# First norm with squares and splits on VectorE alone, in the text's order, and the first two mixer strips part by part together

## The chip, the cores and the metric

The kernel runs on one core of one Trainium2 chip. A core has TensorE (PE, matrix products; PEld loads its weights), VectorE (DVE), ScalarE (ACT), GpSimd (POOL) and SyncE (SP, which here only issues transfers), and 16 DMA engines. The metric is the device time of one execution in microseconds; lower is better. The profile is of one execution taken by the hardware profiler, in us from its first instruction.

## The reference, cut to what matters

One step of a one-layer hybrid decoder for 1024 prompt tokens and 8 × 4 sample tokens with the same weights. The first stages are what the change touches: keys and values of a memory of 256 tokens, the first norm, and the projection of the normed tokens.

```
def rmsnorm(x, g):
    var = jnp.mean(xf * xf, axis=-1, keepdims=True)
    return xf * lax.rsqrt(var + EPS) * g

p_mem_k = jnp.einsum('bmd,lde->lbme', mem_prompt, w_mem_k)
p_mem_v = jnp.einsum('bmd,lde->lbme', mem_prompt, w_mem_v)
...
u = rmsnorm(h, W['norm_mix'][l])
proj = jnp.einsum('bld,de->ble', u, W['w_in'][l])     # columns: pool | z | x,B,C | dt | gate | lru
xbc, new_conv = causal_dwconv(xbc, conv_buf, conv_w, conv_b)   # width 4, then SiLU
...
```

Behind it come three mixers (pooling, a state-space scan, a recurrent block), the output projection, attention to the memory and a SwiGLU layer; the change leaves them as they are.

## The kernel before, in words

**Layout and products.** The 1056 tokens (1024 prompt, 32 sample) lie along the free axis; the 1024 features are 8 tiles of 128 partitions, `xs[0]` to `xs[7]`. The columns are worked in three **parts** `c` of 352. An fp32 operand is split in two fp32r numbers, a high half (a copy on ScalarE) and a low half (the value less the high half, a subtraction elsewhere), and each product becomes three: high·high, high·low, low·high. A **unit** (L146 to L158) is the 8 × 3 products of one strip of 128 output features with one part (or with the memory); it calls `tick()` at its half and at its end, which counts time for work started with `spawn` (generators that go on after so many ticks).

**Memory keys and values.** `w_kv` has 16 weight tiles of 128x1024. `issue` loads one into one of six buffers, `split` makes its halves. Eight key units (the loop over `m`, bank `pk`, then a copy `kt` on ScalarE) use tiles 0 to 7; then eight **value groups** (the loop over `k`, 12 products of 128x512 each) sum into four banks `pvv` with tiles 8 to 15. Ahead of each unit or group `beside(i)` runs: it loads token tile `i − 1`, issues weight tile `i + 5`, splits tile `i + 1`, and squares a token tile: ScalarE makes the square, VectorE or GpSimd adds it to `acc`. After the last square `rstd_all` is spawned: sums of `acc` over the features on TensorE (`pv`, L251), the reciprocal root on VectorE, and transposes (`pb`, L322) that ScalarE copies to `rbc`, the norm factor of each token.

**Norm and splits.** `norm_x(c)` makes for each feature tile of part `c` the normed value in place (L330, VectorE), its high half `uh` (L331, ScalarE) and its low half `ul` (L332; VectorE for even tiles, GpSimd for odd ones). Between part 0 and the others the four banks of values are copied out (`vn`, L388 on ScalarE and L390 on VectorE) and stored (L391, issued by ScalarE).

**Projection.** `xbc_proj` takes the strips of x, B and C in the order 8, 10, 0, 1, 2, 3. For each strip and part there is one unit (bank `mm`, three buffers) and then `conv_unit`: a copy `raw` and a scaled copy `cy` on ScalarE, three steps on VectorE (L503), the tanh on ScalarE. Ahead of strip 8's three units stands `dt_unit`, the time steps: 16 products with `dpad`, L427. Weights of the strips come one ahead (`one_ahead`), with two buffers for the halves and three for what is loaded.

**What sets the order.** TensorE and SyncE run in the order of the program's text all through. VectorE and ScalarE do so up to L382, in the block `kv_order`; elsewhere, and on GpSimd all through, a scheduler orders what is ready in its model.

Of the kernel before, what the change touches and what calls it, by code (L numbers as in the profile page):

```python
# [9 lines left out]
F32 = mybir.dt.float32  # L10
F32R = mybir.dt.float32r
AF = mybir.ActivationFunctionType
OP = mybir.AluOpType
PSUM = bass.MemoryType.PSUM

P = 128
# [3 lines left out]
CW = 352  # L20
NCH = 3
LASTP = SEQ - 2 * CW
DM = 1024
KD = DM // P
# [35 lines left out]
def hybrid_step(ctx, tc, xT, memT, consts_d, masks_d, wbd_d, poolw_d, spool_d, w_kv, w_xbc, w_dt, w_lg, w_pool, w_z, h0_d,  # L60
                w_out1, w_out2, w_q, kc_d, vc_d, w_o, w_gu, w_down,
                yT, ktT, vN, smallo, pssd, sssd):
    nc = tc.nc
# [11 lines left out]
    def nm(s):  # L75
        cnt[0] += 1
        return f"{s}{cnt[0]}"

    def slot(dt=F32, name="s"):
        return sl.tile([P, T], dt, tag="slot", name=nm(name))  # L80
# [5 lines left out]
    def spawn(gen):  # L86
        step(gen)
# [38 lines left out]
    def strips():  # L126

        lists = [(w_xbc[m], DM) for m in (8, 10, 0, 1, 2, 3, 9, 11, 4, 5, 6, 7)]
        lists += [(w_pool[g], DM) for g in range(4)]
        lists += [(w_lg[4 * j + t], DM) for t in range(4) for j in range(2)]  # L130
        lists += [(w_z[m], DM) for m in range(8)]
        lists += [(w_out2[m], DM) for m in range(8)] + [(w_out1[m], DM) for m in range(8)]
        lists += [(w_q[m], DM) for m in range(8)]
        lists += [(w_o[0, m], 512) for m in range(8)]
        yield from one_ahead(lists)
# [9 lines left out]
    weights = strips()  # L145

    def unit(out, w, xs, cols, kk):
        whi, wlo = w
        for k in range(kk):
            a, b = k * P, k * P + P  # L150
            xh, xl = xs[k]
            nc.tensor.matmul(out, whi[:, a:b], xh[:, cols], start=k == 0, stop=False)  # L152
            nc.tensor.matmul(out, whi[:, a:b], xl[:, cols], start=False, stop=False)  # L153
            nc.tensor.matmul(out, wlo[:, a:b], xh[:, cols], start=False, stop=k == kk - 1)  # L154
            if k == kk // 2 - 1:
                tick()
        tick()

    def ch(c):
        return slice(c * CW, (c + 1) * CW)  # L160
# [7 lines left out]
    def cc(name, i=None, n=1):  # L168
        a, b = COFF[name]
        return cst[:, a:b] if i is None else cst[:, a + i:a + i + n]  # L170
# [49 lines left out]
    def square_into(acc, src, first, tmp, eng=nc.gpsimd):  # L220
        if first:
            nc.scalar.activation(acc, src, AF.Square)
        else:
            nc.scalar.activation(tmp, src, AF.Square)
            eng.tensor_tensor(acc, acc, tmp, op=OP.add)
# [11 lines left out]
    tp = mx_.enter_context(tc.tile_pool(name="tp", bufs=2))  # L237
# [3 lines left out]
    def so(name):  # L241
        a, b = SOFF[name]
        return outs[:, a:b]
# [14 lines left out]
    kv_order = ExitStack()  # L258
# [4 lines left out]
    raws = [slot(name="kvw")[:, :DM] for _ in range(6)]  # L263
# [42 lines left out]
    u = []  # L306
    rb0 = slot(name="rbc")
    acc = slot(name="acc")
    xs = []
# [15 lines left out]
    def norm_x(c):  # L325
        if c == 0:
            u.extend((slot(F32R, "uh"), slot(F32R, "ul")) for _ in range(KD))
        for k in range(KD):
            x, (hi, lo) = xs[k][:, ch(c)], u[k]
            nc.vector.scalar_tensor_tensor(x, x, cc("gmix", k), rb0[:, ch(c)], op0=OP.mult, op1=OP.mult)  # L330
            nc.scalar.activation(hi[:, ch(c)], x, AF.Copy)  # L331
            (nc.gpsimd if k % 2 else nc.vector).tensor_tensor(lo[:, ch(c)], x, hi[:, ch(c)].bitcast(F32), op=OP.subtract)  # L332

    def beside(i):

        if 0 <= i - 1 < KD:
            x = slot(name="x")
            nc.sync.dma_start(x, xT[(i - 1) * P:(i - 1 + 1) * P, :])
            xs.append(x)
        if i + 5 < 16:  # L340
            issue(i + 5)
        if i + 1 < 16:
            split(i + 1)
        k = i - 1 - 2
        if 0 <= k < KD:
            square_into(acc, xs[k], k == 0, slot(name="sq") if k else None, nc.vector if k > 4 else nc.gpsimd)
        if k == KD - 1 + 2:
            spawn(rstd_all())

    for m in range(8):  # L350
# [12 lines left out]
    pv = [ps.tile([P, 512], F32, tag="mm", name=nm("pvv"), bufs=3) for _ in range(3)] + [smps(name="pvv")]  # L363
    for k in range(KD):
        beside(8 + k)
        if k == 3:
            nc.sync.dma_start(cst, consts_d)
            nc.sync.dma_start(msk, masks_d)
            nc.sync.dma_start(wdt, w_dt)
        whi, wlo = kvw[8 + k]  # L370
        for i in range(2):
            for j in range(2):
                a, e = slice(i * P, (i + 1) * P), slice(j * 512, (j + 1) * 512)
                hi, lo = mpairs[k]
                nc.tensor.matmul(pv[2 * i + j], hi[:, a], whi[:, e], start=k == 0, stop=False)
                nc.tensor.matmul(pv[2 * i + j], lo[:, a], whi[:, e], start=False, stop=False)
                nc.tensor.matmul(pv[2 * i + j], hi[:, a], wlo[:, e], start=False, stop=k == KD - 1)
        tick()
    nc.scalar.activation(dpad3[:, :, :16], wdt3, AF.Copy)
    nc.vector.tensor_tensor(dpad3[:, :, 32:48], wdt3, dpad3[:, :, :16].bitcast(F32), op=OP.subtract)  # L380
    drain()
    kv_order.close()  # L382
    norm_x(0)
    for i in range(2):
        for j in range(2):
            vn = sd.tile([P, 512], F32, tag="seg", name=nm("vn"), bufs=4)
            if j:
                nc.scalar.activation(vn, pv[2 * i + j], AF.Copy)  # L388
            else:
                nc.vector.tensor_copy(vn, pv[2 * i + j])  # L390
            nc.scalar.dma_start(vN[i * P:(i + 1) * P, j * 512:j * 512 + 512], vn)  # L391
    for c in range(1, NCH):
        norm_x(c)

    def softplus(p, x, n):

# [93 lines left out]

    def conv_unit(c, psum, conv_i, sstate, pout, sout, prev, y):

        raw = tp.tile([P, 3 + CW], F32, tag="raw", name=nm("raw"), bufs=3)
        if c == 0:
            nc.gpsimd.memset(raw[:, :3], 0.0)
        else:
            nc.gpsimd.tensor_copy(raw[:, :3], prev[:, CW:CW + 3])
        w = [cc("conv", conv_i * 5 + j) for j in range(5)]
        n = CW if c < 2 else LASTP
        nc.scalar.activation(raw[:, 3:], psum, AF.Copy)  # L500
        nc.scalar.activation(y, psum, AF.Identity, scale=w[3], bias=w[4])  # L501
        for j in (2, 1, 0):
            nc.vector.scalar_tensor_tensor(y[:, :n], raw[:, j:j + n], w[j], y[:, :n], op0=OP.mult, op1=OP.add)  # L503
        if c == 2:
            rs = tp.tile([P, NB, 7], F32, tag="rs", name=nm("rs"), bufs=2)
            nc.gpsimd.tensor_copy(rs[:, :, 0:3], smp(sstate))
            nc.gpsimd.tensor_copy(rs[:, :, 3:7], smp(raw[:, 3 + n:]))
            for j in (2, 1, 0):
                nc.vector.scalar_tensor_tensor(smp(y[:, n:]), rs[:, :, j:j + 4], w[j], smp(y[:, n:]), op0=OP.mult, op1=OP.add)
            nc.gpsimd.tensor_copy(pout, raw[:, n:n + 3])  # L510
            nc.gpsimd.tensor_copy(smp(sout), rs[:, :, 4:7])
        return raw

    xbc = [None] * 12

    def xbc_proj(tiles):
        for m in tiles:
            w = next(weights)
            xbc[m] = slot(name=f"xbc{m}_")
            raw = None  # L520
            for c in range(NCH):
                if m == 8:
                    dt_unit(c)
                p = mmps()
                unit(p, w, u, ch(c), KD)
                y = tp.tile([P, CW], F32, tag="cy", name=nm("cy"), bufs=5, padded_shape=[P, CY])
                raw = conv_unit(c, p, m, cc("sconv", m * 24, 24), so("psconv")[:, m * 3:m * 3 + 3],
                                so("ssconv")[:, m * 24:m * 24 + 24], raw, y)
                o = xbc[m][:, ch(c)]
                nc.scalar.activation(o, y, AF.Tanh)  # L530
                nc.vector.scalar_tensor_tensor(o, o, 1.0, y, op0=OP.add, op1=OP.mult)
# [321 lines left out]
                if m < 3:  # L853
                    upair(*z_pairs[m], y, "gssd", m, ch(c))

    xbc_proj((8, 10, 0, 1, 2, 3))
    spawn(ssd())
    xbc_proj((9, 11, 4, 5, 6, 7))
    pool()
    lru()  # L860
    z_proj(range(4))
# [32 lines left out]
    for m in range(8):  # L894
        w = next(weights)
        if m < 7:
            nc.sync.dma_start(h[m + 1], xT[(m + 1) * P:(m + 2) * P, :])
        for c in range(NCH):
            p = mmps()
# [9 lines left out]
    u = [(slot(F32R, "uh"), slot(F32R, "ul")) for _ in range(8)]  # L909
# [9 lines left out]
    acc = rp.tile([P, T], F32, tag="acc", name="acc_mem", bufs=1)  # L919
    for m in range(8):  # L920
        w = next(weights)
        for c in range(NCH):
            p = mmps()
# [9 lines left out]
    with ExitStack() as at:  # L933
# [174 lines left out]
        op0 = opairs(0)  # L1108
# [17 lines left out]
        op1 = opairs(1)  # L1126
# [125 lines left out]
    tiles = itertools.count()  # L1252
# [36 lines left out]
    for c in range(2):  # L1289
        for m in range(8):  # L1290
            while len(held) < min(m + 2, 8):
                hold()
            for s in range(2):
                cols = slice(s * TH + c * HB, s * TH + (c + 1) * HB)
                p = mmps()[:, :HB]
                unit(p, held[m], op1, cols, 4)
                nc.vector.tensor_tensor(h[m][:, cols], h[m][:, cols], p, op=OP.add)
            if m:
                sq = fp.tile([P, 2, HB], F32, tag="sq2", name=nm("sq"), bufs=2)
# [82 lines left out]
    hid, ws = [], []  # L1382
# [187 lines left out]
    if True:  # L1570
# [26 lines left out]
        for a, b in LAST:  # L1597
            for m in range(8):
                p = ps.tile([P, b - a], F32, tag="mm", name=nm("mm"), bufs=3)
# [3 lines left out]
                sq = fp.tile([P, b - a], F32, tag="ar", name=nm("sq"), bufs=4, padded_shape=[P, T])  # L1603
# [123 lines left out]
```

## Time and profile before

| | |
|---|---|
| median of 3 runs | 1774.46 us (1774.37 to 1774.67) |
| the profiled execution | 1776.31 us |
| its span, first to last instruction | 1774.5 us |
| TensorE busy | 1718.7 us, 97% |
| its weight loads | 1668.6 us, 94% |
| VectorE busy | 1137.5 us, 64% |
| ScalarE busy | 813.5 us, 46% |
| GpSimd busy | 515.2 us, 29% |
| granted TensorE clock, mean | 0.992 |
| DMA, mean over the span | 111 GB/s |

The shares are averages over stages with different limits. In the rows quoted below a row of the timeline gives start and duration in us, then engine, line, operation, tiles and shapes, how many instructions the row holds (`x2`), and in brackets how long the engine stood idle ahead of it and what released it. A row of the groups gives the total busy time and the mean in ns of one. A matmul's duration reaches into the next one's, so the pace of products is read from the starts.

### The profile page before, as it was taken

Reading aid. Unit: us, or ns where it says so; the run is one execution under the profiler, and the core shown is the slowest. Engines: PE = TensorE matmul, PEld = TensorE weight load, DVE = VectorE, ACT = ScalarE, POOL = GpSimd, SP = SyncE. Lnnn points to the kernel's source line nnn. Section 1 sums busy time; section 2 is a strip of 40 time slices with the busy share of each in tenths; the row PEclk is TensorE's granted clock in tenths of the full one; section 3 lists DMA queues with packets and bytes.
Section 4 is the critical chain, followed back from the end, with each engine's and each line's share of the span. In section 5 each row is a group of like instructions: output and inputs, shape, how many; then the busy total and the mean of one; then the engine's idle time right before and its main releaser. Section 6 shows DMA issues by size and latency. Waiting matters only on the chain.

```text
span 1774.5 us, 31790 instructions
## 1 busy us (share of the span) xinstructions
PE 1718.7 (97%) x12307; PEld 1668.6 (94%) x12307; DVE 1137.5 (64%) x2105; ACT 813.5 (46%) x1650; POOL 515.2 (29%) x516
## 2 busy tenths in 40 slices
PE   8899999999999999999999989999999999899997
PEld 7799998998999999999999989999999999899896
DVE  4887887797744434455566479555555556686855
ACT  6546674687634213355564355223322224353344
POOL 2311114321332322212221244334433332111435
PEclk9999999999999999999999989999999999999999
DMA  9112222341321512243344231232322225543322
GB/s 345 70 44 73 66 70 93 118 141 60 136 77 72 192 62 84 71 152 123 113 146 149 96 134 45 93 116 95 107 91 95 93 91 179 192 169 118 109 72 99
DMA packets 106504, 197.52 MB, mean 111 GB/s; under 512 B 15344, under 2 KB 33392, under 8 KB 106352
## 3 DMA queue, kind: packets, MB, share of 16 engines
q1 hardware_dynamic: 94832, 173.54, 28.9%
q10 hardware_dynamic: 11520, 21.94, 3.4%
q8 instruction: 97, 1.59, 0.4%
q14 instruction: 55, 0.45, 0.1%
HBM read 151.54 MB, written 43.89 MB: 110 GB/s over the span
## 4 chain that ended last, share of the span: by engine, by line
PE 87%; DVE 6%; DMA 2%; ACT 2%; issue 2%; POOL 1%; SPq 0%; ACTq 0%; DVEq 0%; POOLq 0%
PE mm L152 14%; PE mm L154 14%; PE mm L153 14%; PE st L1326 10%; PE st L1327 10%; PE st L1328 10%; PE pss L1065 1%; PE poa L1083 1%; DVE x L330 1%; PE st L1454 1%; PE pdg L596 1%; PE st L1455 1%; PE st L1456 1%; DVE xd L1372 1%; PE psa L1014 1%
## 5 line engine op out<-in xcount | busy, mean ns | idle before, releaser
L152 PE MATMUL mm<-uh,whi 128*128 128x352 f32 x960 | 319.4, 333 | 1.2 <-ACT cy L501 1.1
L1326 PE MATMUL st<-x,whi 128*128 128x264 f32 x1120 | 318.8, 285 | 0.6 <-ACT tm L1506 0.6
L1327 PE MATMUL st<-x,whi 128*128 128x264 f32 x1120 | 318.1, 284 | 0.0
L1328 PE MATMUL st<-x,wlo 128*128 128x264 f32 x1120 | 318.0, 284 | 0.0
L154 PE MATMUL mm<-uh,wlo 128*128 128x352 f32 x960 | 310.0, 323 | 0.0
L153 PE MATMUL mm<-ul,whi 128*128 128x352 f32 x960 | 309.7, 323 | 0.0
L1326 PEld LDWEIGHTS st<-x,whi 128*128 128x128 f32 x1120 | 210.7, 188 | 1.0 <-ACT tm L1506 0.8
L1328 PEld LDWEIGHTS st<-x,wlo 128*128 128x128 f32 x1120 | 210.7, 188 | 0.0
L1327 PEld LDWEIGHTS st<-x,whi 128*128 128x128 f32 x1120 | 210.6, 188 | 0.0
L152 PEld LDWEIGHTS mm<-uh,whi 128*128 128x128 f32 x960 | 180.8, 188 | 5.9 <-issue 1.9
L153 PEld LDWEIGHTS mm<-ul,whi 128*128 128x128 f32 x960 | 181.2, 189 | 2.5
L154 PEld LDWEIGHTS mm<-uh,wlo 128*128 128x128 f32 x960 | 180.6, 188 | 0.0
L1326 PE MATMUL st<-xd,whi 128*128 128x264 f32 x504 | 144.8, 287 | 13.1 <-ACT w L1552 6.5
L1327 PE MATMUL st<-xd,whi 128*128 128x264 f32 x504 | 144.2, 286 | 0.0
L1328 PE MATMUL st<-xd,wlo 128*128 128x264 f32 x504 | 143.8, 285 | 0.0
L1259 ACT ACTIVATE whi<-as 128x512 fp32r<-128x512 f32 (+1 forms) x128 | 74.7, 584 | 140.5 <-PE st L1327 97.8
L1259 ACT ACTIVATE whi<-ar 128x512 fp32r<-128x512 f32 (+1 forms) x104 | 60.8, 588 | 149.7 <-PE st L1327 86.6
L123 ACT ACTIVATE whi<-wraw 128x512 fp32r<-128x512 f32 x128 | 77.7, 627 | 110.9 <-PE mm L153 80.6
L1244 POOL TENSOR_TENSOR as<-ar 128x512 f32<-128x512 f32 (+1 forms) x32 | 53.2, 1663 | 207.6 <-DVE wlo L1260 174.2
L1326 PEld LDWEIGHTS st<-xd,whi 128*128 128x128 f32 x504 | 95.7, 190 | 14.6 <-ACT w L1552 6.7
L124 DVE TENSOR_TENSOR wlo<-wraw,whi 128x512 fp32r<-128x512 f32 x128 | 92.2, 740 | 21.9 <-ACT whi L123 21.8
L1328 PEld LDWEIGHTS st<-xd,wlo 128*128 128x128 f32 x504 | 95.7, 190 | 0.0
(461 smaller groups left out, 4316.3 us busy)
## 6 DMA issues: line engine op xcount, KB each, us to landing
ar<-w_gu SPq DMA_DIRECT2D x88, 256.0 KB, 3.9
hid_dram<-tm SPq DMA_DIRECT2D x71, 264.0 KB, 2.2
xd<-hid_dram SPq DMA_DIRECT2D x63, 264.0 KB, 4.9
ar<-w_down SPq DMA_DIRECT2D x48, 192.0 KB, 3.2
h_dram<-h ACTq DMA_DIRECT2D x16, 528.0 KB, 3.0
h<-h_dram SPq DMA_DIRECT2D x16, 528.0 KB, 6.2
seg<-acs_dram SPq DMA_DIRECT2D x32, 256.0 KB, 3.8
wraw<-w_out SPq DMA_DIRECT2D x32, 256.0 KB, 3.6
```

The source lines that it names most:

```text
L123: nc.scalar.activation(hi[:, a:b], raw, AF.Copy)
L124: nc.vector.tensor_tensor(lo[:, a:b], raw, hi[:, a:b].bitcast(F32), op=OP.subtract)
L152: nc.tensor.matmul(out, whi[:, a:b], xh[:, cols], start=k == 0, stop=False)
L153: nc.tensor.matmul(out, whi[:, a:b], xl[:, cols], start=False, stop=False)
L154: nc.tensor.matmul(out, wlo[:, a:b], xh[:, cols], start=False, stop=k == kk - 1)
L330: nc.vector.scalar_tensor_tensor(x, x, cc("gmix", k), rb0[:, ch(c)], op0=OP.mult, op1=OP.mult)
L596: nc.tensor.matmul(pdg[a:a + 64, b:b + P], xdt[:, h * 64:(h + 1) * 64], segs[h // 4][:, h % 4, :], start=True, stop=True)
L1244: nc.gpsimd.tensor_tensor(s1, a21, a22, op=OP.add)
L1259: nc.scalar.activation(hi[:, a], src, AF.Copy)
L1326: nc.tensor.matmul(out, whi[:, a:b], xh, start=begins and k == 0, stop=False, skip_group_check=True)
L1327: nc.tensor.matmul(out, whi[:, a:b], xl, start=False, stop=False, skip_group_check=True)
L1328: nc.tensor.matmul(out, wlo[:, a:b], xh, start=False, stop=k == kk - 1, skip_group_check=True)
```

## The change

The odd tiles' low halves and the four additions of squares that GpSimd made go to VectorE, which then makes all of them. A tile is squared one step of `beside` sooner, and `rstd_all` is spawned two value groups sooner (two steps less of delay after the eighth square where there were two); the constants, masks and time-step weights are loaded two groups sooner. `norm_x` writes each tile's low half behind the next tile's norm, and VectorE keeps that order (`manual_schedule`). All four value banks are copied by ScalarE. Strips 8 and 10 are worked together: for each part a unit of 8 and one of 10, with four `raw` buffers instead of three; the other strips alone as before.

```diff
--- before.py
+++ after.py
@@ -325,11 +325,14 @@
     def norm_x(c):
         if c == 0:
             u.extend((slot(F32R, "uh"), slot(F32R, "ul")) for _ in range(KD))
-        for k in range(KD):
-            x, (hi, lo) = xs[k][:, ch(c)], u[k]
-            nc.vector.scalar_tensor_tensor(x, x, cc("gmix", k), rb0[:, ch(c)], op0=OP.mult, op1=OP.mult)
-            nc.scalar.activation(hi[:, ch(c)], x, AF.Copy)
-            (nc.gpsimd if k % 2 else nc.vector).tensor_tensor(lo[:, ch(c)], x, hi[:, ch(c)].bitcast(F32), op=OP.subtract)
+        for k in range(KD + 1):
+            if k < KD:
+                x = xs[k][:, ch(c)]
+                nc.vector.scalar_tensor_tensor(x, x, cc("gmix", k), rb0[:, ch(c)], op0=OP.mult, op1=OP.mult)
+                nc.scalar.activation(u[k][0][:, ch(c)], x, AF.Copy)
+            if k:
+                hi, lo = u[k - 1]
+                nc.vector.tensor_tensor(lo[:, ch(c)], xs[k - 1][:, ch(c)], hi[:, ch(c)].bitcast(F32), op=OP.subtract)
 
     def beside(i):
 
@@ -341,10 +344,10 @@
             issue(i + 5)
         if i + 1 < 16:
             split(i + 1)
-        k = i - 1 - 2
+        k = i - 1 - 1
         if 0 <= k < KD:
-            square_into(acc, xs[k], k == 0, slot(name="sq") if k else None, nc.vector if k > 4 else nc.gpsimd)
-        if k == KD - 1 + 2:
+            square_into(acc, xs[k], k == 0, slot(name="sq") if k else None, nc.vector)
+        if k == KD:
             spawn(rstd_all())
 
     for m in range(8):
@@ -363,7 +366,7 @@
     pv = [ps.tile([P, 512], F32, tag="mm", name=nm("pvv"), bufs=3) for _ in range(3)] + [smps(name="pvv")]
     for k in range(KD):
         beside(8 + k)
-        if k == 3:
+        if k == 1:
             nc.sync.dma_start(cst, consts_d)
             nc.sync.dma_start(msk, masks_d)
             nc.sync.dma_start(wdt, w_dt)
@@ -380,17 +383,16 @@
     nc.vector.tensor_tensor(dpad3[:, :, 32:48], wdt3, dpad3[:, :, :16].bitcast(F32), op=OP.subtract)
     drain()
     kv_order.close()
+    kv_order.enter_context(tc.manual_schedule(engines={mybir.EngineType.DVE}))
     norm_x(0)
     for i in range(2):
         for j in range(2):
             vn = sd.tile([P, 512], F32, tag="seg", name=nm("vn"), bufs=4)
-            if j:
-                nc.scalar.activation(vn, pv[2 * i + j], AF.Copy)
-            else:
-                nc.vector.tensor_copy(vn, pv[2 * i + j])
+            nc.scalar.activation(vn, pv[2 * i + j], AF.Copy)
             nc.scalar.dma_start(vN[i * P:(i + 1) * P, j * 512:j * 512 + 512], vn)
     for c in range(1, NCH):
         norm_x(c)
+    kv_order.close()
 
     def softplus(p, x, n):
 
@@ -490,7 +492,7 @@
 
     def conv_unit(c, psum, conv_i, sstate, pout, sout, prev, y):
 
-        raw = tp.tile([P, 3 + CW], F32, tag="raw", name=nm("raw"), bufs=3)
+        raw = tp.tile([P, 3 + CW], F32, tag="raw", name=nm("raw"), bufs=4)
         if c == 0:
             nc.gpsimd.memset(raw[:, :3], 0.0)
         else:
@@ -513,19 +515,20 @@
 
     xbc = [None] * 12
 
-    def xbc_proj(tiles):
-        for m in tiles:
-            w = next(weights)
-            xbc[m] = slot(name=f"xbc{m}_")
-            raw = None
-            for c in range(NCH):
+    def xbc_proj(groups):
+        for ms in groups:
+            ws = [next(weights) for _ in ms]
+            raws = [None] * len(ms)
+            for m in ms:
+                xbc[m] = slot(name=f"xbc{m}_")
+            for c, (n, m) in itertools.product(range(NCH), enumerate(ms)):
                 if m == 8:
                     dt_unit(c)
                 p = mmps()
-                unit(p, w, u, ch(c), KD)
+                unit(p, ws[n], u, ch(c), KD)
                 y = tp.tile([P, CW], F32, tag="cy", name=nm("cy"), bufs=5, padded_shape=[P, CY])
-                raw = conv_unit(c, p, m, cc("sconv", m * 24, 24), so("psconv")[:, m * 3:m * 3 + 3],
-                                so("ssconv")[:, m * 24:m * 24 + 24], raw, y)
+                raws[n] = conv_unit(c, p, m, cc("sconv", m * 24, 24), so("psconv")[:, m * 3:m * 3 + 3],
+                                    so("ssconv")[:, m * 24:m * 24 + 24], raws[n], y)
                 o = xbc[m][:, ch(c)]
                 nc.scalar.activation(o, y, AF.Tanh)
                 nc.vector.scalar_tensor_tensor(o, o, 1.0, y, op0=OP.add, op1=OP.mult)
@@ -853,9 +856,9 @@
                 if m < 3:
                     upair(*z_pairs[m], y, "gssd", m, ch(c))
 
-    xbc_proj((8, 10, 0, 1, 2, 3))
+    xbc_proj(((8, 10), (0,), (1,), (2,), (3,)))
     spawn(ssd())
-    xbc_proj((9, 11, 4, 5, 6, 7))
+    xbc_proj(((9,), (11,), (4,), (5,), (6,), (7,)))
     pool()
     lru()
     z_proj(range(4))
```

TensorE, behind strip 8's first unit (bank `mm` of rows L152 to L154 with weights `whi`, `wlo`). Before:

```order
L154 MATMUL mm_760<-uh_623,wlo_722 128x352
L152 MATMUL mm_760<-uh_625,whi_721 128x352
L153 MATMUL mm_760<-ul_626,whi_721 128x352
L154 MATMUL mm_760<-uh_625,wlo_722 128x352
L427 MATMUL mm_795<-uh_611,dpad_426 128x352
L427 MATMUL mm_795<-ul_612,dpad_426 128x352
L427 MATMUL mm_795<-uh_613,dpad_426 128x352
L427 MATMUL mm_795<-ul_614,dpad_426 128x352
```

After the change:

```order
L154 MATMUL mm_774<-uh_625,wlo_725 128x352
L152 MATMUL mm_774<-uh_627,whi_724 128x352
L153 MATMUL mm_774<-ul_628,whi_724 128x352
L154 MATMUL mm_774<-uh_627,wlo_725 128x352
L152 MATMUL mm_809<-uh_613,whi_734 128x352
L153 MATMUL mm_809<-ul_614,whi_734 128x352
L154 MATMUL mm_809<-uh_613,wlo_735 128x352
L152 MATMUL mm_809<-uh_615,whi_734 128x352
```

Before, the second time-step unit follows, which needs the second part of the columns; now strip 10's unit on the first part does.

VectorE, from the first part's fifth norm step on (`x` are the token tiles, L330 and L331 the norm, L332 and L335 the low halves). Before:

```order
L330 SCALAR_TENSOR_TENSOR x_311<-x_311,cst,rbc_132 128x352
L330 SCALAR_TENSOR_TENSOR x_349<-x_349,cst,rbc_132 128x352
L332 TENSOR_TENSOR ul_616<-x_237,uh_615 128x352
L330 SCALAR_TENSOR_TENSOR x_387<-x_387,cst,rbc_132 128x352
L330 SCALAR_TENSOR_TENSOR x_432<-x_432,cst,rbc_132 128x352
L332 TENSOR_TENSOR ul_620<-x_311,uh_619 128x352
L390 COPY vn_651<-pvv_428 128x512
L390 COPY vn_657<-pvv_430 128x512
L332 TENSOR_TENSOR ul_624<-x_387,uh_623 128x352
```

After the change:

```order
L331 SCALAR_TENSOR_TENSOR x_314<-x_314,cst,rbc_132 128x352
L335 TENSOR_TENSOR ul_620<-x_276,uh_619 128x352
L331 SCALAR_TENSOR_TENSOR x_352<-x_352,cst,rbc_132 128x352
L335 TENSOR_TENSOR ul_622<-x_314,uh_621 128x352
L331 SCALAR_TENSOR_TENSOR x_390<-x_390,cst,rbc_132 128x352
L335 TENSOR_TENSOR ul_624<-x_352,uh_623 128x352
L331 SCALAR_TENSOR_TENSOR x_435<-x_435,cst,rbc_132 128x352
L335 TENSOR_TENSOR ul_626<-x_390,uh_625 128x352
L335 TENSOR_TENSOR ul_628<-x_435,uh_627 128x352
L331 SCALAR_TENSOR_TENSOR x_167<-x_167,cst,rbc_132 128x352
```

Before, odd tiles' low halves are missing here (GpSimd makes them) and two value copies stand between; now all eight low halves stand here, one behind the next norm step, and no value copy.

ScalarE, in the same place (L331 and L332 the high halves, `vn` the value copies, DMA their stores). Before:

```order
L331 ACTIVATE uh_613<-x_202 128x352
L331 ACTIVATE uh_615<-x_237 128x352
L331 ACTIVATE uh_617<-x_273 128x352
L331 ACTIVATE uh_619<-x_311 128x352
L331 ACTIVATE uh_621<-x_349 128x352
L388 ACTIVATE vn_654<-pvv_429 128x512
L331 ACTIVATE uh_623<-x_387 128x352
L391 DMA vN<-vn_651 128x512
L331 ACTIVATE uh_625<-x_432 128x352
L391 DMA vN<-vn_654 128x512
L391 DMA vN<-vn_657 128x512
L388 ACTIVATE vn_660<-pvv_431 128x512
```

After the change:

```order
L332 ACTIVATE uh_617<-x_238 128x352
L391 ACTIVATE vn_653<-pvv_431 128x512
L332 ACTIVATE uh_619<-x_276 128x352
L392 DMA vN<-vn_653 128x512
L332 ACTIVATE uh_621<-x_314 128x352
L391 ACTIVATE vn_656<-pvv_432 128x512
L391 ACTIVATE vn_659<-pvv_433 128x512
L332 ACTIVATE uh_623<-x_352 128x352
L392 DMA vN<-vn_656 128x512
L332 ACTIVATE uh_625<-x_390 128x352
L392 DMA vN<-vn_659 128x512
L332 ACTIVATE uh_627<-x_435 128x352
```

Before, ScalarE makes two value copies, the first behind six of the part's high halves; now it makes four, the first of them ahead of the fourth high half.

## The prediction

> **What bounds the kernel now.** I read the shares of the chain that ended last, then the busy times in five stretches of the front, then each wait of TensorE there.
>
> ```profile
> PE 87%; DVE 6%; DMA 2%; ACT 2%; issue 2%; POOL 1%; SPq 0%; ACTq 0%; DVEq 0%; POOLq 0%
> ```
> ```profile
> core 0: us, PE busy (x) PEld busy (x) DVE busy (x) ACT busy (x) POOL busy (x), PEclk, DMA share, GB/s
> 11.40:36.10 24.70, 23.92 (x179) 23.09 (x180) 11.60 (x9) 15.92 (x20) 9.14 (x4) 1.00 1.01 390
> 36.10:63.40 27.30, 26.42 (x125) 20.55 (x123) 20.89 (x34) 17.59 (x27) 7.99 (x7) 1.00 0.45 164
> 63.40:87.00 23.60, 17.63 (x98) 15.38 (x98) 23.60 (x34) 13.44 (x28) 12.46 (x13) 1.00 0.12 46
> 87.00:110.00 23.00, 21.91 (x140) 21.34 (x139) 20.91 (x68) 10.93 (x24) 3.93 (x14) 1.00 0.13 46
> 110.00:150.00 40.00, 40.00 (x250) 39.59 (x250) 30.15 (x72) 23.88 (x60) 5.41 (x23) 1.00 0.25 75
> ```
>
> TensorE carries 87% of the chain. From 110 us it is busy in all 40.00 of 40.00 us, and both programs' orders agree again from about there; so what TensorE loses before that point is on the path, and what it gains there should reach the end. Between 63.40 and 87.00 the bound is another: VectorE is busy 23.60 of 23.60 us, while TensorE has only 17.63. TensorE's own rows:
>
> ```profile
> 63.18 0.39 PE L377 MATMUL pvv<-kvl,mhi 128*128 128x512 f32 x1
> 65.15 0.40 PE L427 MATMUL mm<-uh,dpad 128*128 128x352 f32 x1 [1.58 <-issue]
> ...
> 69.50 0.43 PE L427 MATMUL mm<-ul,dpad 128*128 128x352 f32 x1 [0.71 <-POOL ul L332]
> 69.77 0.32 PE L152 MATMUL mm<-uh,whi 128*128 128x352 f32 x1
> ...
> 73.63 0.32 PE L427 MATMUL mm<-uh,dpad 128*128 128x352 f32 x1
> ...
> 76.31 0.43 PE L427 MATMUL mm<-ul,dpad 128*128 128x352 f32 x1 [1.70 <-DVE ul L332]
> ...
> 86.67 0.43 PE L427 MATMUL mm<-ul,dpad 128*128 128x352 f32 x1 [0.80 <-POOL ul L332]
> 86.94 0.32 PE L152 MATMUL mm<-uh,whi 128*128 128x352 f32 x1
> ...
> 104.55 0.43 PE L152 MATMUL mm<-uh,whi 128*128 128x352 f32 x1 [1.09 <-ACT cy L501]
> ```
>
> A unit of 24 products takes 73.63 − 69.77 = 3.86 us, 0.161 each; a time-step unit of 16 takes 2.57. From the last value product (63.18, 0.23 to the next) to strip 8's third unit (86.94) stand three time-step units and two strip units: 96 × 0.161 + 0.23 = 15.7 us of work in 23.76 us. **8.1 us are lost there**, waiting for the split input of each third of the columns.
>
> **Why VectorE is late: GpSimd beside it.**
>
> ```profile
> L330 DVE SCALAR_TENSOR_TENSOR x<-x,cst,rbc 128x352 f32<-128x352 f32 x24 | 18.9, 834 | 0.2 <-ACT rbc L323 0.2
> L332 POOL TENSOR_TENSOR ul<-x,uh 128x352 fp32r<-128x352 f32 x12 | 14.9, 1247 | 24.1 <-ACT uh L331 24.1
> ```
> ```profile
> 57.74 2.07 DVE L330 SCALAR_TENSOR_TENSOR x<-x,cst,rbc 128x352 f32<-128x352 f32 x4 [0.23 <-ACT rbc L323]
> ...
> 61.51 2.47 DVE L330 SCALAR_TENSOR_TENSOR x<-x,cst,rbc 128x352 f32<-128x352 f32 x2
> 63.90 0.51 DVE L332 TENSOR_TENSOR ul<-x,uh 128x352 fp32r<-128x352 f32 x1
> ```
> ```profile
> 60.28 3.31 POOL L332 TENSOR_TENSOR ul<-x,uh 128x352 fp32r<-128x352 f32 x2 [13.10 <-ACT uh L331]
> ```
>
> With GpSimd idle four normalising steps take 2.07 us, 0.50 each; while it splits, two take 2.47, 1.24 each. Twelve splits on GpSimd cost VectorE some 24 × (0.83 − 0.50) = 8 us; on VectorE itself they cost 12 × 0.45 = 5.4 us (0.51 a row, 0.07 of it over the next). So the move is worth about 2.6 us of VectorE time over the three parts; the two value copies leave it too.
>
> [...]
>
> **The change, part by part.**
>
> *Squares on VectorE, a step earlier.* Four additions leave GpSimd, where one takes about 3 us, for VectorE, where it takes 1.25:
>
> ```profile
> 29.31 2.98 POOL L225 TENSOR_TENSOR acc<-acc,sq 128x1056 f32<-128x1056 f32 x1 [0.43 <-ACT sq L224]
> ```
> ```profile
> 40.12 1.25 DVE L225 TENSOR_TENSOR acc<-acc,sq 128x1056 f32<-128x1056 f32 x1
> ...
> 48.57 1.28 DVE L124 TENSOR_TENSOR wlo<-wraw,whi 128x512 fp32r<-128x512 f32 x2
> ```
>
> ```profile
> 14.15 0.39 ACT L355 ACTIVATE kt<-pk 128x256 f32<-128x256 f32 x1 [1.84 <-PE pk L154]
> ...
> 26.33 0.38 ACT L355 ACTIVATE kt<-pk 128x256 f32<-128x256 f32 x1
> ...
> 31.26 1.07 ACT L224 ACTIVATE sq<-x 128x1056 f32<-128x1056 f32 x1
> ...
> 36.33 0.38 ACT L355 ACTIVATE kt<-pk 128x256 f32<-128x256 f32 x1 [0.54 <-PE pk L154]
> ```
> ```profile
> 25.32 1.23 DVE L275 TENSOR_TENSOR kvl<-kvw,kvh 128x1024 fp32r<-128x1024 f32 x1 [1.95 <-ACT kvh L274]
> ...
> 31.39 1.99 DVE L275 TENSOR_TENSOR kvl<-kvw,kvh 128x1024 fp32r<-128x1024 f32 x1 [1.42 <-ACT kvh L274]
> ```
> ```profile
> 40.26 0.50 PE L377 MATMUL pvv<-kvl,mhi 128*128 128x512 f32 x1 [0.38 <-DVE kvl L275]
> ```
>
> The first four key units took (26.33 − 14.15) / 4 = 3.04 us each; the last three, with GpSimd adding, (36.33 − 26.33) / 3 = 3.33, since each weight split then takes 1.99 instead of 1.23. Without GpSimd I take 3.04 again: **0.9 us gained**. The wait at 40.26, a split made beside a GpSimd addition, goes too: **0.5**. The added VectorE work, seven additions of 1.25 us where it had three, lies in stretches where VectorE is busy 11.60 of 24.70 us; each stands behind the split that TensorE waits for. If that cover were gone it would cost up to 4 × 1.25 = 5 us.
>
> The price to check is ScalarE, whose queue now holds a square one key unit sooner, ahead of the copy that frees TensorE's bank. The tightest tile:
>
> ```profile
> 23.56 0.38 SPq L338 DMA_DIRECT2D x<-xT  x1
> ```
> ```profile
> x<-xT SPq DMA_DIRECT2D x1, 528.0 KB, 6.5
> ```
>
> The fifth tile lands at 23.56 + 6.5 = 30.06; its square moves to the slot of the fourth, 31.26. That leaves 1.2 us; with ScalarE 0.9 earlier, still 0.3, and the loads behind freed buffers come sooner too. Cost 0; bounds 0 and 1 us.
>
> *Norm factor two value groups earlier.*
>
> ```profile
> 57.11 1.18 ACT L323 ACTIVATE rbc<-pb 128x512 f32<-128x512 f32 x3 [0.34 <-PE pb L322]
> ```
> ```profile
> 57.61 0.50 PE L375 MATMUL pvv<-kvh,mhi 128*128 128x512 f32 x1
> ```
>
> Let T be the end of the value products (63.4 now). Two groups take T − 57.61 = 5.8 us. The factor now comes at T − 6.3; it will come at T − 12. TensorE's total is unchanged. The constants are queued in front of the last value weight, which is split four groups later, 4 × 2.9 = 11.6 us by the same rows: hidden.
>
> *First part.* VectorE's written order between the factor and T holds five normalisings, three value-weight splits (1.23), four mixer splits (1.28 for two), three splits of the part, and a small one of the time-step weight, by its elements like one more of these: 5 × 0.50 + 3 × 1.23 + 4 × 0.64 + 4 × 0.45 = 10.6 us. With an estimated 0.9 of hand-overs to and from ScalarE's halves the fifth normalising ends near T − 0.5. Then ScalarE decides:
>
> ```profile
> L331 ACT ACTIVATE uh<-x 128x352 fp32r<-128x352 f32 x24 | 11.6, 497 | 11.6 <-DVE x L330 9.4 <-PE mm L427 2.2
> ```
> ```profile
> 64.47 0.58 ACT L388 ACTIVATE vn<-pvv 128x512 f32<-128x512 f32 x1
> ...
> 67.16 0.34 ACTq L391 DMA_DIRECT2D vN<-vn  x1
> ```
>
> Its first value copy, ahead of the fourth high half, can only start when that bank's last product is done, near T − 2. In its queue then stand copy 0.6, half 0.45, issue 0.35, half 0.45, two copies 1.2, half 0.45, issue, half, issue, half (1.6): 5.1 us, to T + 3.1; with hand-overs the last split ends at T + 3.8 and the next unit starts at T + 4.1. Unhindered it would be T + 2.6. **1.5 us lost** where before 1.58 for the value copy and more were; bounds 0.3 (ScalarE not in the way) and 3.
>
> *Parts 2 and 3, two units each.* With strip 10 beside strip 8, TensorE has 2 × 3.86 + 2.57 = 10.3 us of work per part. VectorE needs 8 × 0.95 = 7.6 us a part plus convolution steps:
>
> ```profile
> 85.76 3.97 DVE L503 SCALAR_TENSOR_TENSOR cy<-raw,cst,cy 128x352 f32<-128x352 f32 x6
> ```
>
> at 0.66: two in part 2 (8.9 in all), five in part 3 (10.9). Part 2 is split at T + 12.7, wanted at T + 4.1 + 7.7 + 2.3 = T + 14.1. Part 3 at T + 23.6, wanted at T + 24.4. **0 lost**; bounds 0 and 2. Strip 0's weights must now wait for strip 8's third unit, but strip 10's third unit (3.86 us) covers the two splits, 1.28. The wait at 104.55, for a bias copy behind another copy in ScalarE's queue, has the same order and stays.
>
> **Sum.** 8.1 − 1.5 = 6.6 in the normalising stretch, 0.9 and 0.5 ahead of it: 8.0 us. The profiled execution took 1776.31 us, 1.8 of it outside its span of 1774.5; it should become 1768.3, the span 1766.5. The median of the runs, 1774.46, equals that span, so I forecast **1766.5 us**.
>
> **Rivals.**
>
> *ScalarE's queue at T* (chance 0.18). Same mechanism, but halves, copies and issues do not interleave as I laid them out, and parts 2 and 3 lose 1 us each as well: 3 + 2 lost instead of 1.5, 1770. For it: ten instructions stand between the first copy and the last half.
>
> *VectorE stays slow* (0.10). [...] Part 1 then ends 1.6 later; a part takes 10.2 plus convolution, against 10.3 of TensorE work, so parts 2 and 3 lose 1.1 and 2.2. Lost 3.1 + 1.1 + 2.2 = 6.4 of 8.1, gain 3.0 with the front: 1771.5. Against it: the two slow rows stand exactly beside GpSimd's.
>
> *Later stages absorb it* (0.06). If a stage after 150 us is set by something other than TensorE, the 8 us become waits there: 1772 to 1774.5. Against it: 40.00 of 40.00.
>
> *TensorE and ScalarE wait for each other* (0.04, slower). High halves six to eight of each next part stand behind the copies of the unit just running. From that unit's end they and their splits need 3 × (0.50 + 0.45) us and two copies of ScalarE, an estimated 4.2 us; strip 10's unit and the start of the time-step unit give 6. It turns into a loss from 10 us on (two parts, 8 us gained). If each of the three halves waited for a whole unit, 4.2 + 3 × 3.86 = 15.8: 19.6 lost, 1786.
>
> Forecast 0.62, from 1763.5 to 1768.5. The range must leave out at most 0.2: 1763.5 to 1771. A measurement of this kernel can tell about 0.2%, 3.5 us: faster 0.62 + 0.18 = 0.80; same 0.10 + 0.06 = 0.16; slower 0.04.
>
> **What would show it.** Key units at 3.04 us throughout; normalising steps at 0.50, no row at 1.24; TensorE's first time-step unit starting at T without the 1.58 wait, one stretch of waits of 1.5 us before strip 8's first unit at about 66, none in the second and third; strip 8's third unit near 87 although two more units precede it; the wait of about 1.1 near 103. Wrong: squares waiting for input tiles, or high halves behind copies while TensorE idles.

## The result and the profile after

Beside the kernel before on the same chip, the changed kernel took 1766.32 us (median of 6 runs, 1765.48 to 1771.17) against 1774.57 (1774.37 to 1776.6): a ratio of 0.9949, 95% interval 0.994 to 0.9959. A second time, on another occasion, it was 0.9959 (0.9946 to 0.9972). The profiled execution took 1766.45 us, its span 1764.6.

TensorE's rows of the changed kernel (start and duration in us; L429 is now the time-step unit, L152 begins a strip unit) answer to those shown of before:

```profile
60.97 0.39 PE L380 MATMUL pvv<-kvl,mhi 128*128 128x512 f32 x1
61.20 0.32 PE L429 MATMUL mm<-uh,dpad 128*128 128x352 f32 x1
...
63.98 0.43 PE L429 MATMUL mm<-ul,dpad 128*128 128x352 f32 x1 [0.32 <-DVE ul L335]
...
64.89 0.32 PE L152 MATMUL mm<-uh,whi 128*128 128x352 f32 x1
...
72.62 0.33 PE L429 MATMUL mm<-uh,dpad 128*128 128x352 f32 x1
...
75.22 0.32 PE L152 MATMUL mm<-uh,whi 128*128 128x352 f32 x1
...
82.95 0.32 PE L429 MATMUL mm<-uh,dpad 128*128 128x352 f32 x1
...
85.51 0.33 PE L152 MATMUL mm<-uh,whi 128*128 128x352 f32 x1
...
103.16 0.43 PE L152 MATMUL mm<-uh,whi 128*128 128x352 f32 x1 [1.15 <-ACT cy L503]
```

The value products end at T = 61.20 and the first time-step unit starts at once; before it waited 1.58 us, most likely for a bank. Its 16 products take 64.89 − 61.20 = 3.69 us where 2.57 is their work: 1.1 us lost. From there pairs of strip units (72.62 − 64.89 = 7.73, twice 3.86) and time-step units (2.60, 2.56) follow without a gap. **Of the 8.1 us lost before, 1.1 are left.** The wait near 103 us is as it was. The busy times of the stretch around it (TensorE, its loads, VectorE, ScalarE, GpSimd, then the granted clock):

```profile
62.00:86.00 24.00, 23.62 (x145) 22.81 (x144) 23.72 (x50) 16.31 (x35) 1.93 (x6) 1.00 0.12 45
```

VectorE is as full as before, 23.72 of 24.00; but TensorE has 23.62 instead of 17.63 of 23.60. The groups of the norm steps and the low halves (busy time, mean in ns):

```profile
L331 DVE SCALAR_TENSOR_TENSOR x<-x,cst,rbc 128x352 f32<-128x352 f32 x24 | 13.7, 580 | 0.3 <-ACT rbc L323 0.3
L335 DVE TENSOR_TENSOR ul<-x,uh 128x352 fp32r<-128x352 f32 x24 | 12.5, 520 | 0.3
```

0.58 us a norm step, with 0.07 of it over the next instruction, where it was 0.83. And the copies that end the key units:

```profile
25.66 0.38 ACT L358 ACTIVATE kt<-pk 128x256 f32<-128x256 f32 x1
...
35.01 0.39 ACT L358 ACTIVATE kt<-pk 128x256 f32<-128x256 f32 x1 [0.40 <-PE pk L154]
```

The last three units take (35.01 − 25.66) / 3 = 3.12 us instead of 3.33: 0.6 gained. The value products, first to last start, take 60.97 − 34.81 = 26.16 us instead of 63.18 − 36.13 = 27.05: 0.9. The sum is 7.0 + 0.6 + 0.9 = 8.5 us, against 8.3 between the medians. (The span fell by 9.9; 0.7 of that is a first key unit that ended sooner, at 13.45 instead of 14.15 us, ahead of anything that was changed, and about 0.9 appears in the stages behind strip 3, where nothing was changed.)

### The profile page after: what moved, and what is told of

It is laid out like the page before. It is cut to its first block, busy times and chain, and to the rows that moved or that the text cites. A ratio compares the mean times of both kernels' runs of the same rounds, so it can differ in the third digit from the quotient of the medians.

```text
span 1764.6 us, 31762 instructions
## 1 busy us (share of the span) xinstructions
PE 1717.3 (97%) x12307; PEld 1670.0 (95%) x12307; DVE 1133.4 (64%) x2119; ACT 813.4 (46%) x1652; POOL 488.2 (28%) x500
## 5 line engine op out<-in xcount | busy, mean ns | idle before, releaser
L152 PE MATMUL mm<-uh,whi 128*128 128x352 f32 x960 | 319.7, 333 | 1.3 <-ACT cy L503 1.1
L154 PE MATMUL mm<-uh,wlo 128*128 128x352 f32 x960 | 309.9, 323 | 0.0
L152 PEld LDWEIGHTS mm<-uh,whi 128*128 128x128 f32 x960 | 180.8, 188 | 6.0 <-issue 1.9
L154 PEld LDWEIGHTS mm<-uh,wlo 128*128 128x128 f32 x960 | 180.6, 188 | 0.0
L1329 PEld LDWEIGHTS st<-xd,whi 128*128 128x128 f32 x504 | 96.3, 191 | 13.8 <-ACT w L1555 6.7
L1330 PEld LDWEIGHTS st<-xd,whi 128*128 128x128 f32 x504 | 96.4, 191 | 0.0
```

The lines of the kernel that those rows point to most:

```text
L1329: nc.tensor.matmul(out, whi[:, a:b], xh, start=begins and k == 0, stop=False, skip_group_check=True)
L1330: nc.tensor.matmul(out, whi[:, a:b], xl, start=False, stop=False, skip_group_check=True)
```

## The experiments

The runs of the kernel before spread more on these occasions (1769 to 1779 us), so that a ratio is known to about 0.1%, 2 us. Each run is therefore also read by one distance in its profile: **from the first value product to the first product of the state-space scan** (tile `pcb`), behind strip 3, with the same TensorE work between them in all kernels. It is 152.8 − 36.1 = 116.7 us before and 143.8 − 34.8 = 109.0 after; in the second profile of the changed kernel it is 109.0 again. Each distance is that of one execution, and only the changed kernel's was taken twice. It leaves out what differs elsewhere: the profile with squares and factor late has a distance 2.3 us longer than the changed kernel's, but a span of 1764.0 us against 1764.6.

| kernel | distance, us | ratio to before (95%) |
|---|---|---|
| before | 116.7 | 1 |
| before, all low halves on VectorE | 114.6 | 1.0001 (0.9991 to 1.001) |
| before, strips 8 and 10 paired | 124.9 | 1.0046 (1.0033 to 1.006) |
| before, squares and factor early | 124.2 | 1.0046 (1.0033 to 1.006) |
| before, paired, written order | 116.3 | 0.9997 (0.9986 to 1.0008) |
| after | 109.0 | 0.9949 (0.994 to 0.9959) |
| after again | 109.0 | 0.9959 (0.9946 to 0.9972) |
| after, half of the low halves on GpSimd | 112.3 | 0.9969 (0.9957 to 0.9981) |
| after, strips one by one | 115.1 | 0.9993 (0.9982 to 1.0003) |
| after, squares and factor late | 111.3 | 0.997 (0.9961 to 0.998) |
| after, four squares on GpSimd | 108.8 | 0.9955 (0.9942 to 0.9967) |
| after, VectorE's order free | 121.9 | 1.0026 (1.0014 to 1.0038) |
| after, scaled copy first | 107.6 | 0.9954 (0.994 to 0.9969) |
| the same, time steps behind strip 8 | 108.2 | 0.9942 (0.9929 to 0.9956) |

**One part alone, on the kernel before.** First the low halves:

```diff
-            (nc.gpsimd if k % 2 else nc.vector).tensor_tensor(lo[:, ch(c)], x, ...)
+            nc.vector.tensor_tensor(lo[:, ch(c)], x, ...)
```

> The kernel before, with one edit: GpSimd's twelve low halves go to VectorE, the scheduler orders the rest. Theory (GpSimd beside VectorE slows it): normalising steps fall from a mean of 0.83 us to about 0.50 to 0.55, VectorE's total for steps and low halves from 25.3 to 22.8 us, and the stretch from the last value product to strip 8's third unit from 23.8 to about 21.2: 1771.5 to 1772.5. Rival (VectorE is saturated and gets twelve more instructions, no relief): 5.4 us more on the bound, about 1780. Rival (only the order of instructions matters): 1774.5.

The groups of this kernel, then that of VectorE's low halves in the kernel before:

```profile
L330 DVE SCALAR_TENSOR_TENSOR x<-x,cst,rbc 128x352 f32<-128x352 f32 x24 | 13.0, 577 | 0.2 <-ACT rbc L323 0.2
L332 DVE TENSOR_TENSOR ul<-x,uh 128x352 fp32r<-128x352 f32 x24 | 11.7, 517 | 0.1
```
```profile
L332 DVE TENSOR_TENSOR ul<-x,uh 128x352 fp32r<-128x352 f32 x12 | 7.6, 638 | 0.0
```

Twelve instructions more, and VectorE needs less: 24.7 us instead of 18.9 + 7.6 = 26.5. The distance falls by 2.1 us (3.0 up to strip 8's third unit, of which the wait near 103, 1.96 us here, takes back 0.9); the ratio can't tell that from none, but a loss of 5.4 us it rules out. GpSimd's work beside VectorE was the price, not VectorE's own load.

Then the pairing, as in the change's last part, with nothing else:

> The kernel before, with one edit: strips 8 and 10 part by part together. Theory (TensorE gets 10.3 us of work per part where VectorE needs about 8.4 and the convolution steps): the first part's waits of 3.0 us stay, those of the second and third, 5.1 us, go but for about 1.4: 1770 to 1771. Rival (VectorE's total sets the end of the stretch, the pairing only moves the waits): within 1 us of 1774.5. Rival (TensorE and ScalarE wait for each other): above 1776.

It got 8 us **slower**; the one rival that had a loss had another cause for it. The row of TensorE, and the split that it names, of this kernel:

```profile
86.51 0.66 PE L154 MATMUL mm<-uh,wlo 128*128 128x352 f32 x1 [9.75 <-DVE wlo L124]
```
```profile
85.77 0.68 DVE L124 TENSOR_TENSOR wlo<-wraw,whi 128x512 fp32r<-128x512 f32 x1
```

TensorE stands in the middle of strip 10's first unit for the second low half of its weights. In VectorE's order that split has row 81, behind the norm steps of all three parts (rows counted from 0), in this kernel as in the one before; there strip 10 came only behind strip 8's third unit and nobody waited.

The third part alone, the early squares and factor:

```diff
-        k = i - 1 - 2
+        k = i - 1 - 1
...
-        if k == KD - 1 + 2:
+        if k == KD:
...
-        if k == 3:
+        if k == 1:
```

(and all seven additions on VectorE)

> The kernel before, with one edit: all squares added on VectorE and a step sooner, norm factor and constants two groups sooner. Theory: 1.5 us in the key and value products, and of the factor's 5.8 us about 4 in the normalising stretch, whose VectorE work starts sooner: 1768.5 to 1770. Rival (the factor's time is covered by the weight splits anyway, or the stretch is bound by its own work): 1.5 us alone, 1773.

Slower again, by the same thing earlier. TensorE in this kernel:

```profile
79.36 0.66 PE L154 MATMUL mm<-uh,wlo 128*128 128x352 f32 x1 [13.52 <-DVE wlo L124]
```

With the factor there sooner, the scheduler had norm steps ready before the weights, and put the splits of strip 8 itself at rows 81 and 83. The front gained its part: the value products took 26.4 us here.

**One part taken away, from the changed kernel.** The written order of VectorE (the block `manual_schedule` around the norm steps) left out:

```diff
-    kv_order.enter_context(tc.manual_schedule(engines={mybir.EngineType.DVE}))
...
-    kv_order.close()
```

> The changed kernel without the written VectorE order around the norm steps, so that the scheduler orders them. Theory (the written order is what lets the first strips' weight splits stand among the first part's steps; free, they stand behind the steps of all three parts): VectorE does 24 norm steps and 22 low halves, 12 + 10 us, and three value weights, 3.7, ahead of strip 8's low weights, from 50.1 to about 76, and TensorE, which wants them near 65, waits about 11 us, with no later waits for low halves: 1775 to 1778. Rival (the splits on VectorE, the early factor and the pairing carry the gain by themselves): 1766 to 1767.

TensorE and VectorE in this kernel:

```profile
76.78 0.66 PE L154 MATMUL mm<-uh,wlo 128*128 128x352 f32 x1 [12.08 <-DVE wlo L124]
```
```profile
76.03 0.69 DVE L124 TENSOR_TENSOR wlo<-wraw,whi 128x512 fp32r<-128x512 f32 x1
```

The split stands at 76.03, where the theory had 76, and TensorE waited 12.1, where it had 11; by the ratio the time is about 1779, a little above what was expected. In the order that the change writes, the four splits of strips 8 and 10 stand at rows 43 to 53, among the first part's steps. Without that the other parts together are slower than the kernel before.

The strips one after the other again:

```diff
-    xbc_proj(((8, 10), (0,), (1,), (2,), (3,)))
+    xbc_proj(((8,), (10,), (0,), (1,), (2,), (3,)))
```

> The changed kernel, with strips 8 and 10 one after the other again. Theory: VectorE needs 7.6 us and one or two convolution steps a part, TensorE has 6.4 us of work: about 2 us lost in the second part and 3 in the third, 1771 to 1772. Rival (with VectorE relieved and the factor sooner the pairing isn't needed): 1766 to 1767.

6.1 us more in the distance (5.0 expected); by the ratio the time is about 1773, above the 1771 to 1772 expected. TensorE waits in the second and third time-step unit, for one low half after the other:

```profile
70.41 0.43 PE L429 MATMUL mm<-ul,dpad 128*128 128x352 f32 x1 [0.55 <-DVE ul L335]
...
71.34 0.43 PE L429 MATMUL mm<-ul,dpad 128*128 128x352 f32 x1 [0.34 <-DVE ul L335]
...
72.27 0.43 PE L429 MATMUL mm<-ul,dpad 128*128 128x352 f32 x1 [0.35 <-DVE ul L335]
```

One per 0.93 us, VectorE's pace for a norm step and a low half. About 1 us of the 6.1 is clock: between 80 and 86 us it was granted 0.72, and strip 8's third unit with half of the next one took 88.80 − 81.95 = 6.85 us instead of 91.41 − 85.51 = 5.90.

The odd tiles' low halves on GpSimd again, as in the kernel before (the loop writes the low half of tile `k - 1`, so an even `k` stands for an odd tile):

```diff
-                nc.vector.tensor_tensor(lo[:, ch(c)], xs[k - 1][:, ch(c)], ...)
+                (nc.vector if k % 2 else nc.gpsimd).tensor_tensor(lo[:, ch(c)], xs[k - 1][:, ch(c)], ...)
```

> The changed kernel with the odd tiles' low halves on GpSimd again. Theory: norm steps rise to a mean of about 0.83 us, the first part ends 0.8 to 1.5 us later, the second is hidden under TensorE's 10.3 us, the third loses up to 1.4: 1767.5 to 1769.5. Rival (order and pairing cover the splits wherever they are made): 1766 to 1767. Rival (the relief of VectorE carries most of the 8 us): 1771 or more.

3.3 us more in the distance; 0.9969 against 0.9949 and 0.9959 says the same, less sharply. The norm steps are back at a mean of 0.834. The first part lost 2.6 us (67.59 − 62.41 − 2.57) instead of 1.1; the third 0.2; the rest, 1.5, is clock. The view by stretches (TensorE, granted clock, transfers), then products of the unit behind the waits:

```profile
66.00:72.00 6.00, 5.27 (x21) 0.72 0.35 134
67.65:71.05 3.40, 3.40 (x14) 0.50 0.22 82
```
```profile
68.41 0.49 PE L152 MATMUL mm<-uh,whi 128*128 128x352 f32 x1
...
71.22 0.32 PE L153 MATMUL mm<-ul,whi 128*128 128x352 f32 x1
```

Up to 71.05 us a product starts every 0.29 us, behind it every 0.161. So the cover worked in the second and third part even with slow norm steps.

Squares, factor and constants late again (the third part of the change taken back):

> The changed kernel with squares, norm factor and constants as before the change (three squares on VectorE, four on GpSimd, a step later; factor and constants two groups later). Theory: 1.5 us in the key and value products come back, and the first part's norm starts 5.8 us later against products that end at the same distance: 3 to 5 us of waits in front of strip 8's first unit, none in the later parts, 1771 to 1773. Rival (only the 1.5 us of the front): 1768.

2.3 us more in the distance: 0.8 in the value products (27.0 us) and 1.6 in the first part (67.72 − 62.41 − 2.57 = 2.7 lost). I had expected 3 to 5 there. Three of the strips' weight splits, which cost the first part 0.64 us each in the changed kernel, stand here at 47.66 to 53.4 us, when VectorE waited for the factor anyway.

Four additions of squares on GpSimd, still a step sooner:

```diff
-            square_into(acc, xs[k], k == 0, slot(name="sq") if k else None, nc.vector)
+            square_into(acc, xs[k], k == 0, slot(name="sq") if k else None, nc.vector if k > 4 else nc.gpsimd)
```

> The changed kernel with the first four additions of squares on GpSimd again, still a step sooner. Theory: three key units return from about 3.05 to 3.33 us and one value group waits 0.4 us for a weight split made beside an addition: the last value product 1.0 to 1.4 us later, nothing else moves, 0.0006 to 0.0008 above the changed kernel's ratio. Rival (the additions were hidden, what the front gained is the start of the transfers): no difference in the time from the first to the last product of keys and values.

The last three key units took 3.41 us each instead of 3.12, 0.9 in all; the value products took 25.9, as little as in the changed kernel, so that the 0.4 us expected there did not come. The ratio of 0.9955 can't tell this kernel from the changed one. So by the trace the key units gain by the engine and the value products by the earlier step: GpSimd's last addition ends at 36.0 us here, and the split that took 1.89 beside it in the kernel before takes 1.23.

**Does the pairing fail alone by the split's place?** The kernel before, paired, with the changed kernel's loop in the written order, low halves of the odd tiles on GpSimd, squares, factor and value copies as before:

> The kernel before with the pairing, as in the run of the pairing alone, and besides it the changed kernel's loop of norm steps in the written VectorE order; odd tiles' low halves stay on GpSimd in number (the even ones move there instead of the odd ones), squares, factor and value copies stay as before. Theory (the pairing failed alone only by the place of strip 10's second weight split, which the written order puts at row 43 instead of 81): the wait of 9.75 us for it goes, the first part keeps 3 to 4 us of waits, the later parts lose at most 1.5: 1769 to 1771. Rival (the pairing doesn't pay without relief for VectorE or the early factor): 1774 or more.

(The expectation has the tiles wrong: with this loop it is the odd ones that stay on GpSimd.) The 9.75 us are gone, and the distance falls from 124.9 to 116.3. But by the expectation it should have been about 112, and by the ratio of 0.9997 the time is about 1774, where the rival has it: the pairing with the written order alone gains nothing. All that is lost is lost in the first part; the second and third time-step units take 2.58 and 2.56 us, with no loss. VectorE, ScalarE and TensorE in this kernel:

```profile
68.00 1.28 DVE L394 COPY vn<-pvv 128x512 f32<-128x512 f32 x2
68.14 0.58 ACT L392 ACTIVATE vn<-pvv 128x512 f32<-128x512 f32 x1
```
```profile
68.82 0.63 PE L432 MATMUL mm<-uh,dpad 128*128 128x352 f32 x1 [5.02 <-issue]
```

Now the value copies are late: VectorE's, which the written order keeps behind all its steps of the first part, and ScalarE's first, behind all eight high halves. The first time-step unit starts 5.0 us late (1.58 before). The profile names no releaser for it; it starts 0.10 us after the end of that ScalarE copy, as it did in the kernel before (65.05 and 65.15), so a bank that the copies free is what it most likely waited for. Behind that pause the granted clock from 66 to 72 us was 0.59, and the time-step unit and strip 8's first unit took 8.83 us for 6.43 us of products, another 2.4. In the changed kernel, with all four copies on ScalarE, the first starts at 59.30 and this wait doesn't occur; that move was not run by itself.

**What is left.** The wait of 1.15 us near 103 comes from ScalarE's order: three scaled copies (`cy`) stand together behind raw copies of later units. With the two copies of a bank written the other way round:

```diff
-        nc.scalar.activation(raw[:, 3:], psum, AF.Copy)
         nc.scalar.activation(y, psum, AF.Identity, scale=w[3], bias=w[4])
+        nc.scalar.activation(raw[:, 3:], psum, AF.Copy)
```

> The changed kernel with the scaled copy written ahead of the raw copy in each convolution step, so that both of a bank stand together in ScalarE's order. Theory: the wait of 1.15 us near 103 us, where three scaled copies stand behind raw copies of later units, goes; 1.1 us less up to the transpose of the time steps, nothing else. Rival (the time-step activations ahead of them in ScalarE's queue hold the bank as long): no change.

The wait is gone and the distance 1.4 us shorter. The same with each time-step unit behind strip 8's unit (`if m == 10:` instead of `if m == 8:`):

> The same, and each time-step unit behind strip 8's unit instead of ahead of it. Theory: strip 8's unit takes 3.86 us for the eight tiles where the time-step unit takes 2.57, so the first part's tiles, of which the last three came 1.1 us late, come in time: another 1.0 us. Rival (the time steps come one or two units later and what needs them waits): 1 us or more given back between 110 and 160 us.

The first part then loses nothing (strip 8's first unit runs from 60.38 to 64.26, 3.88 us), but a new wait gives it back:

```profile
105.42 0.43 PE L152 MATMUL mm<-uh,whi 128*128 128x352 f32 x1 [1.45 <-ACT raw L503]
```

Copies of three banks stand in ScalarE's queue behind a weight's high half that could not start before 103.84, when TensorE gave its buffer back. Against the changed kernel neither is told apart by its time (0.9954 and 0.9942 against 0.9949 and 0.9959).

## Why the prediction was right, step by step

- **The bound, and what reaches the end.** Right. What TensorE lost ahead of 110 us was on the path: 7.7 us less in the distance, 8.3 in the medians.
- **VectorE slowed by GpSimd.** Right, and shown by one edit alone: 0.834 to 0.577 us a norm step. The sum of 2.6 us was 1.8: the norm steps gave 18.9 − 13.0 = 5.9 us instead of 8, because the mean of 0.83, which counts 0.07 over the next instruction, was set against a pace of 0.50, which doesn't; and the added low halves cost 11.7 − 7.6 = 4.1 instead of 5.4, since those that VectorE had made already took 0.638 us each beside GpSimd and took 0.517 without. The rival without relief had the first of the runs at about 1780; the trace has VectorE's work fall, 26.5 to 24.7 us. It shows that VectorE is slow beside GpSimd; what makes it slow no run shows.
- **Front.** 1.5 us measured, 0.9 + 0.5 predicted, but divided otherwise: 0.6 in the key units, 0.9 in the value products. The key units fell to 3.12, not to 3.04. One term was too high and the other too low; that the sum fits is luck.
- **First part.** 1.1 us lost, 1.5 predicted, and here the step "then ScalarE decides" failed. The first value copy did start before T and ahead of the fourth high half, as laid out:

```profile
59.30 0.60 ACT L391 ACTIVATE vn<-pvv 128x512 f32<-128x512 f32 x1 [1.29 <-PE pvv L380]
59.80 0.49 ACT L332 ACTIVATE uh<-x 128x352 fp32r<-128x352 f32 x1
59.93 0.34 ACTq L392 DMA_DIRECT2D vN<-vn  x1
...
63.52 0.50 ACT L332 ACTIVATE uh<-x 128x352 fp32r<-128x352 f32 x1 [0.58 <-DVE x L331]
```

But the issues of the stores, which the prediction counted one behind the other with the copies and halves at 0.35 us each, ran beside them (59.93 to 60.27, while a half runs from 59.80 to 60.29), and ahead of the eighth high half ScalarE stood idle for 0.58 us until VectorE's norm step was done. VectorE hardly waited for ScalarE. Its rows of the same place:

```profile
58.93 0.68 DVE L124 TENSOR_TENSOR wlo<-wraw,whi 128x512 fp32r<-128x512 f32 x1
...
59.97 0.57 DVE L331 SCALAR_TENSOR_TENSOR x<-x,cst,rbc 128x352 f32<-128x352 f32 x1
...
62.91 0.58 DVE L331 SCALAR_TENSOR_TENSOR x<-x,cst,rbc 128x352 f32<-128x352 f32 x1
63.40 1.17 DVE L335 TENSOR_TENSOR ul<-x,uh 128x352 fp32r<-128x352 f32 x2
```

No row has a bracket. From the fifth norm step's end (60.47, T − 0.7; forecast T − 0.5) eight more steps at 0.47 us, 3.8, end at 64.2 at the soonest; the last low half ended at 64.57. So some 0.4 us are ScalarE's, and the rest is VectorE's own work, with four weight splits ahead of the last steps. No row gives the 0.9 us of hand-overs in the forecast's T − 0.5 or those behind its T + 3.1, which were my estimates: from the first norm step at 50.12 to the fifth's end the one wait in VectorE's rows is 0.44 us, for a value weight's high half. The size came out near by luck. I had taken "unhindered" from the time-step unit's own length and not followed VectorE to the end. That the late factor cost only 1.6 us there, where three of those splits go first, fits this.

- **Second and third part.** 0 lost, as predicted, and the margin was real: with half of the halves on GpSimd the third part lost only 0.2.
- **The wait near 103.** 1.15 measured, "about 1.1" predicted.
- **What the prediction didn't see.** It costed no edit for the written VectorE order, which it found in the changed program's rows and took for granted. Taken away, it costs 12.9 us in the distance, more than the whole gain. The parts are not terms that add up: alone on the kernel before, two of the three lose 7 to 8 us.

Of the rivals, slow norm steps are refuted by the groups, a loss in later stages by the medians, which fell by about as much as the stretch ahead of 110 us gained, and ScalarE's queue by the rows above. TensorE and ScalarE never waited for each other over a whole unit. (The time given for slow norm steps was too low by the prediction's own prices: with five convolution steps a third part of 8 × (0.83 + 0.45) + 5 × 0.66 = 13.5 us against 10.3 loses about 3, not 2.2.)

## What to carry to other kernels

When a queue is full, ask first who slows its instructions: work taken back from an engine beside which its instructions run slowly can shorten it, as twelve more instructions did here (26.5 to 24.7 us). When TensorE's order is changed, look up in the other engines' orders where the new unit's inputs stand, weights too: a split that stood late did no harm until somebody wanted it early. And before a part of a change is called its cause, run it alone; here two of the three parts lose time alone and pay together.

## What was not expected of the hardware

The clock fell to half behind some of TensorE's pauses and not behind others. In the kernel with GpSimd's halves TensorE had 2.57 us of products in the 5.2 us between 62.41 and 67.59, and then ran 3.4 us at 0.29 us a product with a granted clock of 0.50, which cost 1.5 us. With the strips one by one the granted clock was 0.72 from 80 to 86 us, which is again 3.4 us if 0.50 and 1.00 are the only levels in it. In the kernel paired in the written order it was 0.59 from 66 to 72 and 0.88 from 72 to 80, reckoned so 6.8 us, twice that; there TensorE was idle for the whole 5.0 us ahead. In the kernel with squares and factor late, 2.7 lost of 5.3 us cost nothing (1.00 in every stretch from 58 to 100), and the kernel before kept a clock of 1.00 through all its 8.1 us of waits (63.40 to 87.00). Which pauses bring it on was not tried, so the 1 to 2.4 us of clock in these three runs are a cost of their pauses that another execution may not have.
